# Sums of x one or two splits sooner, an earlier stage-end read-out, and a sixth pair of blocks in seven products

## The chip, the cores and the metric

The kernel runs on one core of one Trainium2 chip. The metric is the device time of one execution, in microseconds (us); the kernel is judged by the median of its runs. The engines are called PE (TensorE, matrix products), PEld (its weight loads), DVE (VectorE), ACT (ScalarE), POOL (GpSimd) and SP (SyncE, which issues most transfers).

## The reference

Two layers (DEPTH = 2) of a token mixer work on x of 256 tokens by 2048 channels in float32. Per layer:

```
h = rmsnorm(x, norm_g)
c_a, c_glu, c_gate, q_down, kv_down, k_pe, m_gate, g_conv, g_mla = split(h @ w_in)
y_conv = conv_branch(c_a, c_glu, c_gate, ...) @ w_proj_conv     # GLU, causal depthwise conv, layernorm, silu, gate
y_mla  = mla_branch(q_down, kv_down, k_pe, m_gate, ...) @ w_proj_mla   # low-rank attention, 16 heads, gate
y = sigmoid(g_conv) * y_conv + sigmoid(g_mla) * y_mla
x = x + y @ w_out
```

All that the change touches are the products by `w_proj_conv` and `w_out` (2048 by 2048 each) and what is done to their results.

## The kernel before, in words

**Blocks and splits.** Every weight matrix is cut into blocks of 512 columns (a few are narrower). A stage is named for its matrix: the last stages of a layer are gmla, gconv, pmla, pconv (`w_proj_conv`) and wout (`w_out`), four blocks each. A block of pconv or wout has 2048 rows of weights, in eight pieces of two groups of 128 rows (KS = 2). Float32 accuracy is made out of a faster float format (fp32r): each weight piece `raw` is copied to a rounded high part `hi` by ACT (a CAST), and DVE subtracts to get the low part `lo`; the activations are kept as high and low parts as well. One piece then takes three products (high by high, low of x by high, high of x by low), for two groups of rows and two tiles of 128 tokens: twelve matmuls of 512 columns. This piece of work, the making of its parts with it, is called a split here (a tick in the code). DVE makes low parts two splits ahead of PE, ACT high parts three ahead (LO_AHEAD, HI_AHEAD), and SP loads further ahead into seven `raw` buffers.

**Seven products.** Some pairs of blocks save products. For the first two pieces of both blocks of a pair, that is four weight pieces (b11 and b21 of the left block, b12 and b22 of the right one) and two tiles of tokens, the eight piece-by-tile products are replaced by seven products of sums (Strassen's scheme in Winograd's form). Their weight sides are pieces or sums of pieces: q1 = b11, q2 = b21, q3 = b22, q7 = b12 + b22, q6 and q4 of further sums, q5 = b12 and b11 combined; DVE makes these sums (`sum`, `form`). Their x sides are tiles of x or sums of tiles, called forms in the code: `form_a` and `form_b`. One such product takes six matmuls. The remaining six pieces of each block are plain splits, so a pair has twelve splits, first the left block's and then the right one's; for wout's first pair the order alternates by twos. The set SEVEN names the pairs: pconv 2 (that is blocks 2 and 3), wout 0 and wout 2, in both layers, without wout 2 in the last layer: five pairs. A pair's products are spread out by `plan_all`: q1, q7, q6 and q5 go ahead of the splits that lie 7, 5, 3 and 2 from the end of the block or pair before it (TAIL), and q2, q4 and q3 ahead of splits 0, 2 and 4 of the pair itself.

**The order of the work.** Each engine's order is fixed by hand: the class `InOrder` chains every instruction to the one issued before it on its engine. `product` walks through a block's splits. For each it issues the products of the seven that stand there, prepares parts of coming weights (`prepare`), issues the twelve matmuls and then calls `background`, which counts a clock of splits up by one and issues all steps that are due. `at_slot(n, f)` makes f due n splits later, and there is no waiting for a step's data in it: a step that is issued with its data not there holds up its engine's queue.

**The sums of x.** `make_forms` plans four steps: `whole` (DVE adds high and low parts to whole numbers, two adds, tiles `whole_a` and `whole_b`), one split later `differences` (four DVE subtractions), one later `separate` (ACT's high parts of the forms) and one later DVE's low parts. `forms_at` says when the first is due, in splits from the start of the block in which the seven begin: `ticks + TAIL[ticks][1] - 3`, where `TAIL[ticks][1]` is the place of q7, the first that needs a form. For a block of eight splits that is 0, for a pair of twelve it is 4. It is called once for each stage and layer: for pconv (whose products begin in pconv block 1, of eight splits) and for wout (which begin in the pconv pair, of twelve), so four times in all. Where the number is 0 or less, the steps are planned one block sooner, during the block before.

**The read-out.** A finished block is read out of the accumulators by an evacuation function (`pconv_evac`, `wout_evac`), issued as a step of `background`. If a pair of seven products begins inside the block (`planned.begins`), the two token tiles are read out at EVAC_AT = 1 split after the last one and one later; otherwise both are read out together, EVAC_AT splits after the last one, or at `evac_at` for the last half of a block or pair. `evac_at` was 0 for `i == 3`, a block that a pair of seven products never has as its own index. In `pconv_evac` and `wout_evac` (layer 0) a result is then turned: written to DRAM in strips (`park`, on POOL's queue, for the last block's second tile on SP's), fetched back (`fetch`, POOL) and transposed in blocks by DVE, at fixed numbers of splits after the read-out, and split into high and low parts for the next stage (`yT`, `hT`). In the last layer `wout_evac` adds x and sends the result to the output.

**The end.** The last block of the last layer, wout 3, has eight plain splits in `last_product`: the two last splits are reordered so that token tile 0 finishes first and is read out, then tile 1 without its last piece, and this last piece is made in two halves of 256 columns in banks of their own (`acc_end`), each added and sent off as soon as it is there. x for a block comes by `wout_begin`, at the block's start, or for the second block of a pair at slot 8.

Of the kernel before, what the change touches and what calls it, by code (L numbers as in the profile page):

```python
# [11 lines left out]
F32 = mybir.dt.float32  # L12
# [57 lines left out]

REVOLUTION_PIECES = 6

SEVEN = {(l, kind, i) for l in range(DEPTH) for kind, i in (("pconv", 2), ("wout", 0), ("wout", 2))} - {(DEPTH - 1, "wout", 2)}


def revolution_pieces():
# [43 lines left out]
def trunk(ctx: ExitStack, tc: tile.TileContext, xT, x, g_in, pos, win, wuq, wukv, wpc, wpm, wo, cst, rows, invf, out):  # L120
# [281 lines left out]
            return high(0, 0) + high(1, 0) + low(0) + low(1) + high(0, 1) + high(1, 1)  # L402
        return [e for t in two for p in two for e in high(t, p)] + low(0) + low(1)

    def last_product(planned, stat, first_out, early_out, half_out):

        nk, n, mine = planned.nk, planned.n, [tick[-1][1] for tick in planned.ticks]
        blocks_begun[0] += 1
        own, other = blocks_begun[0] % 2, 1 - blocks_begun[0] % 2
        pts = [acc_p.tile([P, 512], F32, tag=f"acc{own}{t}", name=f"acc{mine[0]}_{t}") for t in range(T)]  # L410
        ends = [acc_p.tile([P, 256], F32, tag=f"acc{other}{a}", name=f"acc{mine[0]}_end{a}") for a in range(2)]

        def products(j, t, dst, cols, begin, end):
            hi, lo, _ = done[mine[j]]
            terms = [(kk, p) for p in range(2) for kk in range(KS)] + [(kk, 2) for kk in range(KS)]
            for m, (kk, part) in enumerate(terms):
                sh, sl = stat(j * KS + kk, t)
                stationary, w = ((sh, hi), (sl, hi), (sh, lo))[part]
                pe.matmul(
                    dst, stationary, w[:, kk, cols],  # L420
                    start=begin and m == 0, stop=end and m == len(terms) - 1,
                )

        whole = slice(0, n)
        for j, i in enumerate(mine):
            prepare(i)
            if j < len(mine) - 2:
                for t, kk, part in order_of_products(i, False, False):
                    k = j * KS + kk
                    sh, sl = stat(k, t)  # L430
                    stationary, w = ((sh, done[i][0]), (sl, done[i][0]), (sh, done[i][1]))[part]
                    pe.matmul(pts[t], stationary, w[:, kk, :], start=k == 0 and part == 0, stop=False)
            elif j == len(mine) - 2:
                products(j, 0, pts[0], whole, False, False)
                products(j + 1, 0, pts[0], whole, False, True)
                first_out(pts[0])
                products(j, 1, pts[1], whole, False, True)
                early_out(pts[1])
            else:
                for a in range(2):  # L440
                    products(j, 1, ends[a], slice(256 * a, 256 * a + 256), True, True)
                    half_out(a, ends[a])
            background(n)

    def prepare(i):
        for a in range(HI_AHEAD + 1):
            split_hi(i + a)
            if a <= LO_AHEAD:
                split_lo(i + a)
        form(i + HI_AHEAD + 1)  # L450
# [85 lines left out]
        at_slot(begin + 2, separate, 0.0, 1.0)  # L536
        return forms

    def product(planned, stat, evacuate, evac_at=EVAC_AT, costs=(0.0, 0.0), before=None, tardy=None):
        nk, n = planned.nk, planned.n  # L540
        seven = planned.seven
        if seven:
            dst = [[seven.banks[q] for q in qs] for qs in (("q1", "q7"), ("q6", "q5"))]
        else:
            dst = [accumulators(f"acc{planned.pieces[0]}")]

        def evac(right, ts=range(T)):
            for t in ts:
                evacuate(*((right,) if seven else ()), t, dst[right][t][:, : 2 * n] if n == PAIRED else dst[right][t][:, :n])

        ends = {}
        for at, tick in enumerate(planned.ticks):
            ends[tick[-1][0]] = at
        for at, tick in enumerate(planned.ticks):
            for q, i, of in tick[:-1]:
                prepare(i)
                one_of_seven(q, i, of)
            right, i, j = tick[-1]
            pts = dst[right]
            final = at == ends[right]  # L560
            prepare(i)
            hi, lo, _ = done[i]
            if before:
                before(j)
            begins = j == 0 and not seven
            for t, kk, part in [(t, kk, p) for t in range(T) for p in range(2) for kk in range(KS)] if n == PAIRED else ():
                k = j * KS + kk
                pe.matmul(
                    pts[t][:, : (n if part else 2 * n)], stat(k, t)[part], hi[:, kk, :] if part else pairs_of[i][:, kk, :],
                    start=k == 0 and part == 0, stop=k == nk - 1 and part == 1,  # L570
                )
            for t, kk, part in () if n == PAIRED else order_of_products(i, final, j == tardy):
                k = j * KS + kk
                sh, sl = stat(k, t)
                stationary, w = ((sh, hi), (sl, hi), (sh, lo))[part]
                pe.matmul(
                    pts[t][:, :n], stationary, w[:, kk, :],
                    start=begins and kk == 0 and part == 0, stop=k == nk - 1 and part == 2,
                    skip_group_check=seven is not None,
                )  # L580
            if final and planned.begins:
                half = tuple(c / 2 for c in costs)
                for t in range(T):
                    steps.insert(t, (clock[0] + 1 + EVAC_AT + t, half, lambda right=right, t=t: evac(right, [t])))
            elif final:
                steps.insert(0, (clock[0] + 1 + (EVAC_AT if at < len(planned.ticks) - 1 else evac_at), costs, lambda right=right: evac(right)))
            background(n, [u for _, u, _ in tick[:-1]])
# [203 lines left out]
    for l in range(DEPTH):  # L791
# [660 lines left out]
        def add_out(t, c, s, ps, xt, engine):  # L1452
            vec.tensor_add(xt[:, s], ps, xt[:, s])
            engine.dma_start(out[t, :, c * 512 + s.start : c * 512 + s.stop], xt[:, s])

        def wout_end(pl, stat, c=3, keep=keep, add_out=add_out):
            xts = [keep.pop(("x", c, t)) for t in range(T)]
            halves = [slice(a, a + 256) for a in (0, 256)]

            last_product(  # L1460
                pl, stat,
                lambda ps: add_out(0, c, slice(0, 512), ps, xts[0], sp),
                lambda ps: vec.tensor_add(xts[1], ps, xts[1]),
                lambda a, ps: add_out(1, c, halves[a], ps, xts[1], (act, sp)[a]),
            )

        def wout_evac(c, t, ps, keep=keep, l=l, last_layer=last_layer):
# [41 lines left out]
        for at_block, (kind, i, pl) in enumerate(planned):  # L1509
# [4 lines left out]

            def forms_at(b):
                ticks = len(planned[b][2].ticks)
                return ticks + TAIL[ticks][1] - 3

            of, after = pl.begins, at_block + 1 + bool(pl.seven)
            if of:  # L1520
# [49 lines left out]
            elif kind == "mgate":  # L1570
                product(pl, uses_h, lambda t, ps, i=i: mgate_evac(i, t, ps), costs=(0.0, 3.5))
            elif kind == "gmla":
                product(pl, uses_h, lambda t, ps, i=i: gmla_evac(i, t, ps), costs=(0.0, 2.7))
            elif kind == "pmla":
                product(pl, stat_of(*keep["o"]), lambda t, ps, i=i: pmla_evac(i, t, ps), costs=(1.25, 0.0))
            elif kind == "gconv":
                product(pl, uses_h, lambda t, ps, i=i: gconv_evac(i, t, ps), costs=(0.0, 3.9))
            elif kind == "cgate":
                product(pl, uses_h, lambda t, ps, i=i: cgate_evac(i, t, ps), costs=(0.0, 2.0))
            elif kind == "pconv":  # L1580
                while "yc" not in keep:
                    run_fill()
                product(pl, stat_of(*keep["yc"]), evac_of(pconv_evac, i, pl), 0 if i == 3 else EVAC_AT, (2.4, 0.0),
                        before=before_pconv if i == 0 else None)
            else:
                if i:
                    wout_begin(i)
                else:
                    at_slot(5, lambda f=wout_begin: f(0))
                if pl.seven:  # L1590
                    at_slot(8, lambda i=i, f=wout_begin: f(i + 1))
                if last_layer and i == 3:
                    wout_end(pl, stat_of(*keep["y"]))
                    continue
                product(pl, stat_of(*keep["y"]), evac_of(wout_evac, i, pl),
                        0 if i == 3 else EVAC_AT, (1.25, 1.5), tardy=6 if i == 0 else None)
        if not last_layer:
            h_hi, h_lo = keep["h"]

# [105 lines left out]
```

## Time and profile before

| | |
|---|---|
| median of 3 runs | 1876.45 us (1876.35 to 1877.25) |
| the profiled execution, its own time | 1876.67 us |
| its span, first to last instruction | 1874.8 us |
| granted TensorE clock, mean | 1.000 |
| instructions | 26919 |
| DMA | 445.03 MB, mean 237 GB/s |

The profile is of one execution. The share of busy time of an engine is an average; PE's is taken with modelled ends of its matmuls, which overlap, so that the starts of matmuls tell more than their ends. A row of a timeline reads: start, duration of the group, engine, line, operation, result<-operands and shape, how many, and in brackets the idle time of the engine before it with what ended it. All instructions have the line L131, that of the helper which records the order of issue; one goes by the tiles' names. `acc`, `left` and `right` are accumulators (the latter two of the blocks of a pair), `hT`, `ycT` and `yT` the inputs of the stages that read h, the conv branch and y.

### The profile page before, as it was taken

The page shows a single profiled execution, that of the slowest core. Times are in us where ns is not written, and L with a number is a line of the kernel's source. Part 1 is how long each engine was busy: PE and PEld are TensorE (multiplying, and loading weights), DVE is VectorE, ACT ScalarE, POOL GpSimd, SP SyncE. Part 2 cuts the span into 40 slices and gives each one's busy share as a digit, 9 for nine tenths or more (in the row PEclk, how much of TensorE's full clock was granted, in tenths as well). Part 3 has the DMA queues.
Part 4 walks back from the last instruction along what each step waited for, and adds up shares of the span by engine and source line. Part 5 has one row for each costly group of instructions (what it writes and reads, how often), then busy time and mean ns, then how long its engine had stood idle before and what let it go on. Part 6 is the DMA issues. An engine that isn't in the chain of part 4 may idle for free.

```text
span 1874.8 us, 26919 instructions
## 1 busy us (share of the span) xinstructions
PE 1863.2 (99%) x8419; PEld 1550.6 (83%) x8419; DVE 1657.2 (88%) x2560; ACT 1370.2 (73%) x2454; POOL 493.1 (26%) x942
## 2 busy tenths in 40 slices
PE   9999999999999999999999999999999999999999
PEld 8888888888888888778888888888888888887787
DVE  6999998898999999899769998888899999896974
ACT  7678888888887766555657689788889877564552
POOL 0155555542200000111421555555322000001210
PEclk9999999999999999999999999999999999999999
DMA  8777877887765566577977787777877556665684
GB/s 330 237 262 254 270 251 246 269 275 226 241 204 195 194 215 213 179 230 251 315 251 233 257 269 261 254 252 259 270 229 248 193 195 206 197 220 190 221 292 139
DMA packets 138959, 445.03 MB, mean 237 GB/s; under 512 B 23680, under 2 KB 29056, under 8 KB 138816
## 3 DMA queue, kind: packets, MB, share of 16 engines
q1 hardware_dynamic: 104976, 359.50, 57.9%
q0 software_dynamic: 32832, 82.62, 13.7%
q8 instruction: 66, 1.08, 0.2%
q10 hardware_dynamic: 1008, 1.20, 0.2%
q14 instruction: 77, 0.63, 0.1%
HBM read 399.18 MB, written 44.04 MB: 236 GB/s over the span
## 4 chain that ended last, share of the span: by engine, by line
PE 98%; DMA 1%; DVE 1%; issue 0%; POOL 0%; ACT 0%; DVEq 0%; POOLq 0%
PE acc L131 84%; PE left L131 6%; PE right L131 5%; PE o_ps L131 1%; PE s1w L131 1%; PE s L131 1%; DMA turned<-turn_d 0%; DVE sum L131 0%; DMA turn_d<-xres 0%; DMA gx<-in_g 0%; DMA x_in<-in_xT 0%; DVE lo L131 0%; DVE form_a L131 0%; POOL turn_d L131 0%; PE acc_end L131 0%
## 5 line engine op out<-in xcount | busy, mean ns | idle before, releaser
L131 ACT CAST hi<-raw 128x1024 fp32r<-128x1024 f32 (+2 forms) x683 | 698.9, 1029 | 354.4 <-PE acc L131 241.8
L131 DVE TENSOR_TENSOR lo<-raw,hi 128x1024 fp32r<-128x1024 f32 (+2 forms) x667 | 802.2, 1205 | 125.6 <-PE acc L131 62.7
L131 PE MATMUL acc<-hi,hT 128*128 128x512 f32 (+1 forms) x1728 | 422.0, 384 | 0.5 <-ACT hT L131 0.5
L131 PEld LDWEIGHTS acc<-hi,hT 128*128 128x128 f32 x1728 | 319.5, 188 | 64.6 <-ACT hT L131 0.9
L131 PE MATMUL acc<-hi,h_hi 128*128 128x512 f32 (+1 forms) x864 | 264.2, 387 | 0.4 <-ACT h_hi L131 0.4
L131 PE MATMUL acc<-hi,h_lo 128*128 128x512 f32 (+2 forms) x864 | 260.0, 382 | 0.0
L131 ACT ACTIVATE tap<-u_t,cst 128x256 f32<-128x256 f32 x522 | 227.4, 499 | 4.4 <-DVE v_t L131 3.9
L131 PE MATMUL acc<-lo,h_hi 128*128 128x512 f32 (+1 forms) x832 | 224.6, 386 | 0.0
L131 PE MATMUL acc<-lo,hT 128*128 128x512 f32 (+1 forms) x832 | 224.0, 386 | 0.0
L131 POOL DMA_DIRECT2D turned<-turn_d x88 | 49.3, 561 | 535.8 <-DVE v_t L131 337.6
L131 DVE SCALAR_TENSOR_TENSOR v_t<-u_t,cst,v_t 128x256 f32<-128x256 f32 x438 | 187.5, 479 | 2.4
L131 PEld LDWEIGHTS acc<-hi,h_lo 128*128 128x128 f32 x864 | 161.5, 188 | 32.9 <-DVE h_lo L131 0.2
L131 DVE TENSOR_TENSOR v_t<-v_t,tap 128x512 f32<-128x512 f32 x261 | 179.5, 688 | 8.5
L131 PEld LDWEIGHTS acc<-hi,h_hi 128*128 128x128 f32 x864 | 160.1, 188 | 31.4 <-ACT h_hi L131 0.8
L131 POOL DMA_DIRECT2D turn_d<-gate x184 | 100.1, 551 | 317.1 <-DVE gate L131 202.4
L131 PEld LDWEIGHTS acc<-lo,h_hi 128*128 128x128 f32 x832 | 155.1, 188 | 31.5 <-DVE lo L131 0.3
L131 PEld LDWEIGHTS acc<-lo,hT 128*128 128x128 f32 x832 | 155.2, 188 | 31.1
L131 PE MATMUL acc<-hi,oT 128*128 128x512 f32 x512 | 127.8, 389 | 0.0
L131 PE MATMUL acc<-hi,qkc 128*128 128x512 f32 x448 | 115.4, 389 | 0.0
L131 PEld LDWEIGHTS acc<-hi,oT 128*128 128x128 f32 x512 | 95.8, 188 | 19.7
L131 PEld LDWEIGHTS acc<-hi,qkc 128*128 128x128 f32 x448 | 83.6, 188 | 17.0
L131 POOL DMA_DIRECT2D turn_d<-su x128 | 69.9, 552 | 99.6 <-DVE su L131 89.4
(242 smaller groups left out, 2436.1 us busy)
## 6 DMA issues: line engine op xcount, KB each, us to landing
raw<-in_win SPq DMA_DIRECT2D x397, 512.0 KB, 4.3
raw<-in_wpm SPq DMA_DIRECT2D x64, 512.0 KB, 3.4
raw<-in_wpc SPq DMA_DIRECT2D x64, 512.0 KB, 3.4
raw<-in_wo SPq DMA_DIRECT2D x64, 512.0 KB, 4.9
raw<-in_wukv SPq DMA_DIRECT2D x32, 512.0 KB, 4.3
turned<-turn_d POOLq DMA_DIRECT2D x56, 256.0 KB, 4.9
raw<-in_wuq SPq DMA_DIRECT2D x24, 512.0 KB, 4.5
turn_d<-qk POOLq DMA_DIRECT2D x128, 96.0 KB, 3.8
```

Source lines behind the costliest of these rows:

```text
L131: ins = getattr(self.engine, name)(*a, **k)
```

## The change

Three edits. First, `forms_at` gives a number two lower for a block of eight splits (-2 in place of 0) and one lower for a pair of twelve (3 in place of 4). Second, `evac_at` is 0 where `i + bool(pl.seven) == 3`, so for the last pair of a stage too. Third, wout 2 of the last layer joins SEVEN as a sixth pair; since `last_product` knew only plain blocks, its ending becomes a function `closing` that `product` calls for the last two splits, with the same three kinds of pieces and the two halves in the banks `acc00` and `acc01`.

```diff
-SEVEN = {(l, kind, i) for l in range(DEPTH) for kind, i in (("pconv", 2), ("wout", 0), ("wout", 2))} - {(DEPTH - 1, "wout", 2)}
+SEVEN = {(l, kind, i) for l in range(DEPTH) for kind, i in (("pconv", 2), ("wout", 0), ("wout", 2))}
...
-    def last_product(planned, stat, first_out, early_out, half_out):
...
+    def closing_of(stat, first_out, early_out, half_out):
+
+        def closing(step, last_two, pts):
+            pieces = [(done[i], j) for _, i, j in last_two]
...
+            whole = slice(0, 512)
+            if step == 0:
+                products(pieces[0], 0, pts[0], whole, False, False)
+                products(pieces[1], 0, pts[0], whole, False, True)
                 first_out(pts[0])
+                products(pieces[0], 1, pts[1], whole, False, True)
                 early_out(pts[1])
             else:
+                halves = [acc_p.tile([P, 256], F32, tag=f"acc0{a}", name=f"acc_end{a}") for a in range(2)]
                 for a in range(2):
+                    products(pieces[1], 1, halves[a], slice(256 * a, 256 * a + 256), True, True)
+                    half_out(a, halves[a])
...
+            if closing and at >= len(planned.ticks) - 2:
+                prepare(i)
+                closing(at - len(planned.ticks) + 2, [tick[-1] for tick in planned.ticks[-2:]], pts)
+                background(n)
+                continue
...
             def forms_at(b):
                 ticks = len(planned[b][2].ticks)
-                return ticks + TAIL[ticks][1] - 3
+                return ticks + TAIL[ticks][1] - (5 if ticks == 8 else 4)
...
-                product(pl, stat_of(*keep["yc"]), evac_of(pconv_evac, i, pl), 0 if i == 3 else EVAC_AT, (2.4, 0.0),
+                product(pl, stat_of(*keep["yc"]), evac_of(pconv_evac, i, pl), 0 if i + bool(pl.seven) == 3 else EVAC_AT, (2.4, 0.0),
...
-                if last_layer and i == 3:
-                    wout_end(pl, stat_of(*keep["y"]))
-                    continue
-                product(pl, stat_of(*keep["y"]), evac_of(wout_evac, i, pl),
-                        0 if i == 3 else EVAC_AT, (1.25, 1.5), tardy=6 if i == 0 else None)
+                stat = stat_of(*keep["y"])
+                product(pl, stat, evac_of(wout_evac, i, pl), 0 if i + bool(pl.seven) == 3 else EVAC_AT, (1.25, 1.5),
+                        tardy=6 if i == 0 else None, closing=wout_end(stat) if last_layer and i + bool(pl.seven) == 3 else None)
```

More of the change, by code (lines that the diff above doesn't have):

```diff
@@ L403, in order_of_products @@
         return [e for t in two for p in two for e in high(t, p)] + low(0) + low(1)
-    def last_product(planned, stat, first_out, early_out, half_out):
[L407 to L435, printed above, removed]
@@ new lines, in closing_of, with products @@
+    def closing_of(stat, first_out, early_out, half_out):
+        def closing(step, last_two, pts):
+            pieces = [(done[i], j) for _, i, j in last_two]
+            def products(piece, t, dst, cols, begin, end):
+                (hi, lo, _), j = piece
+                terms = [(kk, p) for p in range(2) for kk in range(KS)] + [(kk, 2) for kk in range(KS)]
+                for m, (kk, part) in enumerate(terms):
+                    sh, sl = stat(j * KS + kk, t)
+                    stationary, w = ((sh, hi), (sl, hi), (sh, lo))[part]
+                    pe.matmul(
+                        dst, stationary, w[:, kk, cols],
+                        start=begin and m == 0, stop=end and m == len(terms) - 1, skip_group_check=not begin,
+                    )
+            whole = slice(0, 512)
+            if step == 0:
+                products(pieces[0], 0, pts[0], whole, False, False)
+                products(pieces[1], 0, pts[0], whole, False, True)
@@ L436, in last_product @@
                 first_out(pts[0])
-                products(j, 1, pts[1], whole, False, True)
+                products(pieces[0], 1, pts[1], whole, False, True)
                 early_out(pts[1])
             else:
+                halves = [acc_p.tile([P, 256], F32, tag=f"acc0{a}", name=f"acc_end{a}") for a in range(2)]
                 for a in range(2):
-                    products(j, 1, ends[a], slice(256 * a, 256 * a + 256), True, True)
-                    half_out(a, ends[a])
-            background(n)
+                    products(pieces[1], 1, halves[a], slice(256 * a, 256 * a + 256), True, True)
+                    half_out(a, halves[a])
@@ L445, in prepare @@
+        return closing
     def prepare(i):
@@ L537, in make_forms, with product @@
         return forms
-    def product(planned, stat, evacuate, evac_at=EVAC_AT, costs=(0.0, 0.0), before=None, tardy=None):
+    def product(planned, stat, evacuate, evac_at=EVAC_AT, costs=(0.0, 0.0), before=None, tardy=None, closing=None):
         nk, n = planned.nk, planned.n
@@ L1454, in add_out, with wout_end @@
             engine.dma_start(out[t, :, c * 512 + s.start : c * 512 + s.stop], xt[:, s])
-        def wout_end(pl, stat, c=3, keep=keep, add_out=add_out):
-            xts = [keep.pop(("x", c, t)) for t in range(T)]
+        def wout_end(stat, c=3, keep=keep, add_out=add_out):
             halves = [slice(a, a + 256) for a in (0, 256)]
[L1460 to L1464, printed above, removed]
+            xt = lambda t: keep["x", c, t]
+            return closing_of(
+                stat,
+                lambda ps: add_out(0, c, slice(0, 512), ps, xt(0), sp),
+                lambda ps: vec.tensor_add(xt(1), ps, xt(1)),
+                lambda a, ps: add_out(1, c, halves[a], ps, xt(1), (act, sp)[a]),
             )
```

## The prediction

> **What bounds the kernel now.** I read the page first, then the engine waits of PE, then the timeline around each wait.
>
> ```profile
> span 1874.8 us, 26919 instructions
> ...
> PE 1863.2 (99%) x8419; PEld 1550.6 (83%) x8419; DVE 1657.2 (88%) x2560; ACT 1370.2 (73%) x2454; POOL 493.1 (26%) x942
> ...
> PEclk9999999999999999999999999999999999999999
> ...
> PE left L131 <- DVE form_a L131: 6.6, 4, 2.1
> ...
> PE acc L131 <- ACT hT L131: 0.5, 1, 0.5
> PE acc L131 <- ACT h_hi L131: 0.4, 1, 0.4
> ```
>
> The reader is to see three things. PE is busy for 1863.2 of 1874.8 us and its granted clock is full in every slice, so time comes off only by fewer matmuls or fewer stalls of PE. The list of stalls is short: four of them, 6.6 us together, on `form_a`, a sum of x for the seven products; one of 0.5 us on `hT`, the input of layer 1; one of 0.4 us at the start. DVE and ACT have 88% and 73%, so they matter only where they hand something to PE late. A stall costs more than its listed idle time, because the modelled ends of the matmuls hide a part, so I price stalls by starts of matmuls. First the unit, from the timeline of the pconv pair of layer 0:
>
> ```profile
> 825.83 1.98 PE L131 MATMUL left<-hi,ycT 128*128 128x512 f32 x8
> ...
> 828.55 1.07 PE L131 MATMUL right<-hi,form_b 128*128 128x512 f32 x4
> ...
> 832.63 1.07 PE L131 MATMUL left<-hi,yT 128*128 128x512 f32 x4
> ...
> 833.99 1.52 PE L131 MATMUL left<-hi,ycT 128*128 128x512 f32 x6
> ```
>
> A plain split, twelve matmuls of 512 columns, runs from 825.83 to 828.55: 2.72 us, 0.227 us a matmul. One of the seven products, six matmuls, runs from 832.63 to 833.99: 1.36 us. Any longer stretch of the same count is a stall.
>
> **Part 1, the sums of x sooner.** In the timeline ahead of the pconv pair of layer 0 (the products are begun inside pconv block 1, eight splits):
>
> ```profile
> 777.50 1.23 DVE L131 TENSOR_TENSOR lo<-raw,hi 128x1024 fp32r<-128x1024 f32 x1 [1.50 <-PE acc L131]
> ...
> 784.08 0.69 DVE L131 TENSOR_TENSOR whole_a<-ycT,ycT 128x512 f32<-128x512 f32 x1
> ...
> 790.59 0.42 DVE L131 TENSOR_TENSOR whole_b<-whole_a,whole_b 128x256 f32<-128x256 f32 x1
> ...
> 792.31 1.22 DVE L131 TENSOR_TENSOR lo<-raw,hi 128x1024 fp32r<-128x1024 f32 x1
> ...
> 794.01 1.07 PE L131 MATMUL acc<-lo,ycT 128*128 128x512 f32 x4
> ...
> 794.92 0.61 PE L131 MATMUL left<-hi,form_a 128*128 128x512 f32 x2
> ...
> 796.85 0.68 DVE L131 TENSOR_TENSOR form_a<-whole_a,form_a 128x512 fp32r<-128x512 f32 x1
> ...
> 797.59 0.73 PE L131 MATMUL left<-hi,form_a 128*128 128x512 f32 x2 [2.05 <-DVE form_a L131]
> ...
> 798.62 1.99 PE L131 MATMUL acc<-hi,ycT 128*128 128x512 f32 x8
> ```
>
> Product q7 starts at 794.92 with the high part of `form_a`, waits for the low part, which DVE begins only at 796.85, and the next split starts at 798.62: 3.70 us in place of 1.36, a loss of 2.34. The plan put that subtraction into the background of the split just ahead of q7, at the end of a DVE queue that was still working. And for wout, ahead of its first pair (begun inside the pconv pair, twelve splits):
>
> ```profile
> 839.24 0.69 DVE L131 TENSOR_TENSOR gate<-left,sc 128x512 f32<-128x512 f32 x1
> 839.43 0.61 PE L131 MATMUL left<-hi,form_a 128*128 128x512 f32 x2
> ...
> 840.57 0.68 DVE L131 TENSOR_TENSOR form_a<-whole_a,form_a 128x512 fp32r<-128x512 f32 x1
> ...
> 841.31 0.73 PE L131 MATMUL left<-hi,form_a 128*128 128x512 f32 x2 [1.27 <-DVE form_a L131]
> ...
> 842.34 1.99 PE L131 MATMUL right<-hi,ycT 128*128 128x512 f32 x8
> ```
>
> From 839.43 to 842.34 are 2.91 us in place of 1.36, a loss of 1.55. Here DVE first reads out the left half (`gate`, from 839.24) and only then makes the low part. Layer 1 has the same two places: the four stalls of the list are 6.6 us, twice 2.05 + 1.27. So sums of x cost PE 2 x (2.34 + 1.55) = 7.8 us.
>
> With the change the four steps (add, differences, high parts, low parts) keep their distance to each other and come two splits sooner in the first place, one in the second. First place: the low parts are now due one split after pconv block 0, behind that block's read-out, where the differences stand today; they are two subtractions of 0.68 in place of four of 0.42. By today's clock that queue would be through with them at about 792.0 (790.59 + 1.4), and q7 asks with its third matmul, at 795.37, so 3 us are to spare and all 2.34 go. The adds and differences move into the last three splits of pconv block 0, where DVE idles 1.50 us before a low part (row 777.50); two adds of 0.69 and four differences of 0.42 nearly fit in that, and what doesn't is drawn from the lead of two splits with which low parts are made. Second place: the low parts move ahead of the low part of the next weight, the sum for q6 and the read-out, 1.2 + 1.2 + 1.3 us of queue; they would begin about 836.9 (840.57 less 3.7) and be done about 838.2, 1.7 us before q7's third matmul at 839.88, so all 1.55 go. I charge nothing for the moved steps: they are the same instructions, none of them issues a DMA, and POOL's and SP's queues are not passed. If that cover failed, the price is the rival below.
>
> What is late next? In the first place the low part of the weight ahead of q7 (792.31 + 1.22 = 793.53) is used at 794.01, 0.48 us later; it gains 0.3, since shorter work stands ahead of it. In the second place DVE is nearly full until the end of the pair:
>
> ```profile
> 836.00:872.00 36.00, 34.73 (x153) 28.45 (x152) 34.91 (x41) 19.24 (x22) 8.79 (x16) 1.00 0.69 215
> ...
> 867.62 2.35 DVE L131 TENSOR_TENSOR lo<-raw,hi 128x1024 fp32r<-128x1024 f32 x2
> ...
> 871.37 1.07 PE L131 MATMUL right<-lo,yT 128*128 128x512 f32 x4
> ```
>
> 34.91 of 36 us are busy, so DVE will not run sooner when PE does, and each margin behind the stall shrinks by 1.55. The thinnest that I find is a low part done at 868.84 (867.62 + 1.22) and used at 871.37: 2.53 falls to 1.0, still positive.
>
> The Trainium skill ("TensorE: Matmul & The Clock Gate", the queue depths under the array's architecture) says that VectorE is a strict first-in first-out queue while PE may pull weight loads ahead. The rows agree for VectorE: the subtraction at 840.57 stood behind the read-out at 839.24 though its inputs were long there. Taken alone that rule speaks against the change too, as every step put ahead delays all behind it; it is the first rival.
>
> **Part 2, the read-out at the stage's end.** The argument that becomes 0 is used only where no seven-product pair follows; behind the pconv pairs the other branch with its fixed distance is taken, and the last layer has its own ending. So one place moves: the end of wout in layer 0.
>
> ```profile
> 937.55 1.98 PE L131 MATMUL acc<-hi,hT 128*128 128x512 f32 x8
> ...
> 938.95 1.28 DVE L131 TENSOR_TENSOR xres<-right,xres 128x512 f32<-128x512 f32 x2
> ...
> 952.31 0.71 DVE L131 STREAM_TRANSPOSE turned<-turned 128x512 f32<-128x512 f32 x1 [2.40 <-DMA turned<-turn_d]
> ...
> 953.87 0.61 PE L131 MATMUL acc<-hi,hT 128*128 128x512 f32 x2
> ...
> 954.95 0.79 PE L131 MATMUL acc<-hi,hT 128*128 128x512 f32 x2 [0.46 <-ACT hT L131]
> ...
> 960.28 1.98 PE L131 MATMUL acc<-hi,hT 128*128 128x512 f32 x8
> ```
>
> The read-out (938.95) starts a chain through DRAM that ends in transposes at 952.31 and in `hT`, for which PE waits at 954.95. The two splits from 953.87 to 960.28 take 6.41 us, 0.97 over 2 x 2.72. The read-out moves ahead of one low part, to the end of PE's last split, behind which layer 1 starts at 937.55: some 1.4 us sooner; the parks on POOL and SP and the fetch on POOL move with it. The 2.40 us for which DVE stands at the transpose get longer by about 1, with low parts of weights queued behind, but these have two splits of lead. Bounds: 0.97 gained, or as much lost if those low parts come late. I take 0.9 gained.
>
> **Part 3, the sixth pair.** Seven products in place of eight: 42 matmuls for 48, 6 x 0.227 = 1.36 us less of PE. By the Trainium skill (the same page, "Wait — 56ns, not 53.3ns?") a warm matmul of 512 columns takes 215.7 ns start to start; by that it would be 1.29, and the 0.227 of the rows decides. DVE and ACT get more work there: three more low parts and four sums of 1.22 us (row 877.21), and four joins of about 0.69 (as the read-out at 839.24): 11.3 us.
>
> ```profile
> 1828.00:1868.00 40.00, 40.00 (x178) 33.14 (x177) 19.77 (x22) 13.16 (x13) 4.26 (x8) 1.00 0.48 149
> ...
> 877.21 1.23 DVE L131 TENSOR_TENSOR sum<-raw,raw 128x1024 f32<-128x1024 f32 x1 [2.10 <-DMA raw<-in_wo]
> ...
> 880.09 1.21 DVE L131 TENSOR_TENSOR lo<-sum,hi 128x1024 fp32r<-128x1024 f32 x1
> ...
> 884.06 0.61 PE L131 MATMUL left<-lo,form_a 128*128 128x512 f32 x2
> ...
> raw<-in_wo SPq DMA_DIRECT2D x64, 512.0 KB, 4.9
> ...
> xres<-x_dram SPq DMA_DIRECT2D x8, 256.0 KB, 6.3
> ...
> DMA to landing us min/median/max: 1.9/4.8/10.4
> ```
>
> DVE is busy for 19.77 of 40 us in the last 40 us of today's plain blocks; 11.3 us more fit. The ending itself has the same matmuls (twelve whole, six whole, twelve halves) in banks that are free by then: 0. One step is new on the path: x for the last block is asked for at slot 8, three splits or 8.2 us ahead of the first read-out. The median landing is 6.3 us, the longest of `xres` 10.4: 0 to 2.2 us of cost, and I take 0, as SP issues ahead of PE.
>
> **The sum.** 7.8 + 0.9 + 1.4 = 10.1 us. The profiled execution took 1876.67 us (span 1874.8 and 1.9 around it): 1866.6. The median of the runs is 0.2 lower: 1866.4.
>
> **The rivals.** (1) The stall moves to a weight's low part in the pconv pairs. For: DVE at 34.91 of 36. Against: 1.0 us of margin is left. If the margin is overdrawn, at most 1.55 in each layer comes back: 1866.4 + 3.1 = 1869.5. Chance 0.11. (2) The change doesn't do what it says: the steps are due sooner in the plan, but DVE, being behind, reaches them no sooner. For: its load. Against: two read-outs and weights are passed in the queue itself. Only parts 2 and 3 would count: 1876.4 - 2.3 = 1874.1, no measurable change. Chance 0.05. (3) Slower: the new pair starves for weights. Its first sum needs two pieces of block 3 during block 1. In layer 0 that sum already waited 2.10 us for `raw` (877.21); its low part was done at 881.30 and used at 884.06, 2.8 us later. If in the last layer, where x and out travel too, all four extra pieces landed one after the other, that is 4 x 4.9 = 19.6 us, 16.8 beyond the margin: 1883.2. It outweighs the gain from 10.1 us beyond the margin on. Against: layer 0 has the same loads at the same distance, with the next layer's behind them, and PE did not wait. Chance 0.04.
>
> **The numbers.** 0.80 for the forecast, whose own range is 1865.4 to 1868.6 (1.0 below for the spread of the runs shown, 1876.35 to 1877.25, and 2.2 above for x). With the first rival the range is 1865.4 to 1870.0. A measurement of this kernel tells about 0.2%, 3.75 us, from no change; the forecast and rival (1) lie beyond it: faster 0.91, same 0.05, slower 0.04.
>
> **What would show it.** Right: the line `form_a` is gone from PE's waits, each q7 takes 1.36 us from start to start, PE has 8413 matmuls, and the two splits that took 6.41 take about 5.5. Wrong: PE waits on `lo` from DVE between the sums and the end of the pconv pairs (rival 1), still on `form_a` (rival 2), on `lo` or a sum behind `raw` in the last 50 us (rival 3), or DVE's last additions wait for `xres`.

## The result, and the profile after

The changed kernel takes 1866.8 us (median of 4 runs, 1866.56 to 1867.27) against 1876.85 us of the kernel before in the same session (4 runs, 1876.35 to 1877.98). The ratio is 0.9946, with a 95% interval of 0.9929 to 0.9963: faster by about 10 us, 0.5%. The forecast was 1866.4. The profiled execution took 1866.75 us. In one later session a single execution of the kernel before took 3822.62 us, about twice as long as every other one, and no ratio and no count below contains it.

The page of the changed kernel, and below it its list of PE's waits (us in total, times, longest):

```profile
span 1865.0 us, 26913 instructions
...
PE 1859.9 (100%) x8413; PEld 1549.2 (83%) x8413; DVE 1666.2 (89%) x2571; ACT 1372.7 (74%) x2459; POOL 495.9 (27%) x942
```

```profile
PE right L131 <- DVE xres L131: 0.8, 1, 0.8
PE warm L131 <- PEq L1687: 0.8, 1, 0.8
PE acc L131 <- ACT hi L131: 0.2, 1, 0.2
```

PE has six matmuls fewer, `form_a` and `hT` are gone from its waits, and one line is new: the right block of a pair waits for `xres`. First the place where the sums of x were late, ahead of the pconv pair of layer 0, in the timeline of the changed kernel:

```profile
789.30 0.69 DVE L131 TENSOR_TENSOR gate<-gate,ym 128x512 f32<-128x512 f32 x1
789.91 0.69 DVE L131 TENSOR_TENSOR form_a<-whole_a,form_a 128x512 fp32r<-128x512 f32 x1
...
794.24 1.07 PE L131 MATMUL left<-hi,form_a 128*128 128x512 f32 x4
...
795.14 0.62 PE L131 MATMUL left<-lo,form_a 128*128 128x512 f32 x2
795.60 0.62 PE L131 MATMUL acc<-hi,ycT 128*128 128x512 f32 x2
...
833.61 0.68 DVE L131 TENSOR_TENSOR form_a<-whole_a,form_a 128x512 fp32r<-128x512 f32 x1
...
836.39 1.07 PE L131 MATMUL left<-hi,form_a 128*128 128x512 f32 x4
...
837.30 0.62 PE L131 MATMUL left<-lo,form_a 128*128 128x512 f32 x2
837.75 1.07 PE L131 MATMUL right<-hi,ycT 128*128 128x512 f32 x4
```

The low part of `form_a` now stands right behind the read-out (`gate`) and is done at 790.60; q7 asks for it with its third matmul, at 794.69, 4 us later. q7 runs from 794.24 to 795.60, 1.36 us, where it took 3.70. The second place, ahead of wout's first pair, has the low part done at 834.29, and q7 runs from 836.39 to 837.75, again 1.36. In layer 1 both places look the same.

The end of layer 0, same view:

```profile
932.96 1.30 PE L131 MATMUL acc<-hi,hT 128*128 128x512 f32 x5
933.15 1.29 DVE L131 TENSOR_TENSOR xres<-right,xres 128x512 f32<-128x512 f32 x2 [1.49 <-PE right L131]
...
946.72 0.71 DVE L131 STREAM_TRANSPOSE turned<-turned 128x512 f32<-128x512 f32 x1 [3.81 <-DMA turned<-turn_d]
...
949.27 1.07 PE L131 MATMUL acc<-hi,hT 128*128 128x512 f32 x4
...
954.74 1.52 PE L131 MATMUL acc<-hi,hT 128*128 128x512 f32 x6
```

The read-out comes 0.19 us behind the start of layer 1, before it was 1.40. DVE stands 1.4 us longer at the transpose (3.81 for 2.40), and the two splits from 949.27 to 954.74 take 5.47 us in place of 6.41: no wait is left. And the end of the kernel, same view:

```profile
1857.18 0.61 PE L131 MATMUL right<-lo,yT 128*128 128x512 f32 x2
1857.83 0.69 DVE L131 TENSOR_TENSOR xres<-right,xres 128x512 f32<-128x512 f32 x1 [4.16 <-PE right L131]
...
1858.58 1.19 PE L131 MATMUL right<-hi,yT 128*128 128x512 f32 x4 [0.78 <-DVE xres L131]
...
1861.70 0.42 DVE L131 TENSOR_TENSOR xres<-acc_end,xres 128x256 f32<-128x256 f32 x1 [0.22 <-PE acc_end L131]
```

This is the new line of the waits. Two matmuls begin at 1857.18 and the next ones at 1858.58: 1.40 us for 0.45, with 0.11 more in the first matmul behind it: 1.05 us lost. PE goes on when DVE has read token tile 0 out, though it next writes token tile 1.

**Where the 9.8 us of the span come from.** One stretch belongs to no edit: the start. The same group of matmuls, ahead of any edited work, begins 0.68 us later in the profile of before than after; first before, then after:

```profile
741.88 1.98 PE L131 MATMUL acc<-hi,oT 128*128 128x512 f32 x8
```

```profile
741.20 1.98 PE L131 MATMUL acc<-hi,oT 128*128 128x512 f32 x8
```

From there to the end of the span it is 1132.9 us before and 1123.8 after, a gain of 9.1: 7.78 from q7, 0.97 from `hT`, 1.36 from six matmuls, less 1.05 at the end, which is 9.06.

### The profile page after: what moved, and what is told of

Its sections match the earlier page's. It is cut to its first block, busy times and chain, and to the rows that moved or that the text cites. A ratio compares the mean times of both kernels' runs of the same rounds, so it can differ in the third digit from the quotient of the medians.

```text
span 1865.0 us, 26913 instructions
## 1 busy us (share of the span) xinstructions
PE 1859.9 (100%) x8413; PEld 1549.2 (83%) x8413; DVE 1666.2 (89%) x2571; ACT 1372.7 (74%) x2459; POOL 495.9 (27%) x942
## 4 chain that ended last, share of the span: by engine, by line
PE 100%; DMA 0%; DVE 0%; ACT 0%; issue 0%
PE acc L131 83%; PE left L131 7%; PE right L131 7%; PE o_ps L131 1%; PE s1w L131 1%; PE s L131 1%; DMA raw<-in_win 0%; PE acc_end L131 0%; DVE xres L131 0%; ACT hi L131 0%; PE var L131 0%; PE mu L131 0%
```

## The experiments

Two sessions were run, on different chips, each with the kernel before beside the experiments. The theory is the prediction's three parts, and for the end of the kernel this: the right block's two accumulators are one double PSUM tile (`pair`), so that the order of issue makes the writing of tile 1 wait for the reading of tile 0. The rivals are in each expectation.

**One part alone (e1_sums, e2_readout, e3_sixth).** The kernel before with the first edit; the kernel before with the second; the changed kernel with these two put back.

```diff
e1_sums (kernel before)
-                return ticks + TAIL[ticks][1] - 3
+                return ticks + TAIL[ticks][1] - (5 if ticks == 8 else 4)
e2_readout (kernel before; wout's line, and the same in pconv's)
-                        0 if i == 3 else EVAC_AT, (1.25, 1.5)
+                        0 if i + bool(pl.seven) == 3 else EVAC_AT, (1.25, 1.5)
e3_sixth (changed kernel: these lines as before)
```

> The kernel before with the sums of x sooner and nothing else. Theory (the four stalls on form_a were all of it, and nothing takes their place): 7.8 us less than before, no line form_a among PE's waits, the wait of 0.5 us on hT still there. Rival (the changed kernel owes part of this to the other two edits, or the stalls come back on the low parts of weights): less than 6 us, and PE waits on lo.

> The kernel before with the stage-end read-out in the last split and nothing else. Theory: only the read-out of wout's last pair in layer 0 moves, the wait on hT goes, 0.9 to 1.0 us less; the four waits on form_a stay at 6.6 us. Rival (the longer stand of DVE at the transpose makes low parts of weights late): the time is the same or up to 1 us more, and PE waits on lo near the start of layer 1.

> The change with the sums of x and the read-out put back: the sixth pair with its ending alone. Theory (six matmuls less are 1.36 us, the new wait on xres at the end takes 1.05 back): 0.3 us less than before, with a wait PE right <- DVE xres of 0.8 us. Rival (the wait at the end comes from the other edits): 1.4 us less, and no such wait.

Measured, against a kernel before of 1877.36 us: e1 1868.43 us (1867.93 to 1868.80), ratio 0.9954 (0.9941 to 0.9967); e2 1876.49 (1874.96 to 1877.24), ratio 0.9995 (0.9986 to 1.0004); e3 1876.75 (1875.11 to 1879.47), ratio 0.9999 (0.9990 to 1.0008). PE's waits of e1, then of e3:

```profile
PE acc L131 <- ACT hT L131: 0.6, 1, 0.6
```

```profile
PE left L131 <- DVE form_a L131: 6.6, 4, 2.1
PE right L131 <- DVE xres L131: 0.8, 1, 0.8
```

e1 loses `form_a` and keeps `hT`; e2 loses `hT` and keeps `form_a` (6.6 us); e3 keeps `form_a` and has the new `xres`. One line doesn't fit: e3 reads out as late as before and yet has no line `hT`. It still loses something there, by starts of matmuls 0.47 us over the same two splits, where before loses 0.97 and e1 1.33. DVE's stand at the transpose, which the way through DRAM ends, goes with it, 1.90, 2.40 and 2.86 us; e3's row, then e1's:

```profile
953.20 0.71 DVE L131 STREAM_TRANSPOSE turned<-turned 128x512 f32<-128x512 f32 x1 [1.90 <-DMA turned<-turn_d]
```

```profile
948.49 0.71 DVE L131 STREAM_TRANSPOSE turned<-turned 128x512 f32<-128x512 f32 x1 [2.86 <-DMA turned<-turn_d]
```

From the read-out to this transpose it takes 12.9 us in e3, 13.4 in before and 13.8 in e1. So the loss at `hT` differs between executions, with the time that the way through DRAM takes; why that differs is open.

By the same group of matmuls as above (741.51 in e1) the rest of e1's span is 1867.0 - 741.5 = 1125.5 us, 7.4 less than before. By starts of matmuls e1 gains 3.9 us in each layer at the sums of x, and gives 0.4 to 0.5 back at its longer wait for `hT`; so the theory's 7.8 holds. In e2's profile the two splits take 5.44 us, nothing over 2 x 2.72. The medians of e2 and e3 do not tell half a microsecond, because their executions spread over 2 to 4 us, while those of e1 lie within 0.9. What spreads them shows in e2's profile: a stretch at a lower clock. Its timeline behind the first stall, and its windows ahead of, behind and well behind it (the number after the busy times is the granted clock):

```profile
796.86 0.74 PE L131 MATMUL left<-hi,form_a 128*128 128x512 f32 x2 [2.05 <-DVE form_a L131]
...
798.15 3.33 PE L131 MATMUL acc<-hi,ycT 128*128 128x512 f32 x8
801.32 1.09 PE L131 MATMUL acc<-lo,ycT 128*128 128x512 f32 x4
```

```profile
790.00:796.00 6.00, 4.81 (x22) 3.65 (x20) 5.90 (x8) 2.58 (x4) 4.36 (x8) 1.00 0.63 160
797.70:801.20 3.50, 3.50 (x10) 2.75 (x9) 3.12 (x3) 1.03 (x1) 0.56 (x1) 0.53 0.91 328
802.00:806.00 4.00, 4.00 (x19) 3.30 (x18) 1.97 (x2) 1.67 (x2) 0.00 (x0) 1.00 0.63 210
```

The eight matmuls from 798.15 take 3.17 us; in the profile of before the same eight, behind the same stall of 2.05, take 1.82. The matmuls begin 0.427 us apart for 3.4 us, in place of 0.227: eight of them cost 1.6 us more. In e3's profile it happened behind both stalls of 2.05. Of 34 executions of the kernel before in the two sessions, 12 have a mean clock of 1.000 and take 1875.47 to 1876.32 us, 19 have 0.999 and take 1877.15 to 1878.66, 3 have 0.998 and take 1879.10 to 1879.36. Of these only the mean clock is known. By an estimate from e2's profile, a stretch of 3.4 us at a clock of 0.53 takes 0.0009 off the mean, so 0.999 is read here as one such stretch and 0.998 as two. Among the executions with a mean clock of 1.000, e2 takes 1874.96 to 1875.15, 0.7 to 0.9 less than the mean of before's, 1875.86 (0.9 was the term), and e3 1875.11 to 1876.25, on the mean 0.4 less (1.36 less 1.05 would be 0.3). That fits the two terms; it does not prove them to a tenth.

**The end of the kernel (e4_two_tiles, e7_late_first).** The changed kernel with the right block's two accumulators in two PSUM tiles and the left block's in the double one; and with the accumulators as they are, but the read-out of token tile 0 issued behind the products of tile 1.

```diff
e4_two_tiles
-            pair = tp_p.tile([P, 2, 512], F32, tag="tp", name="right")
-            c12, c22 = pair[:, 0], pair[:, 1]
-            c11 = s_p.tile([P, 512], F32, tag="s0", name="left0")
-            c21 = extra_p.tile([P, 512], F32, tag="extra", name="left1")
+            pair = tp_p.tile([P, 2, 512], F32, tag="tp", name="left")
+            c11, c21 = pair[:, 0], pair[:, 1]
+            c12 = s_p.tile([P, 512], F32, tag="s0", name="right0")
+            c22 = extra_p.tile([P, 512], F32, tag="extra", name="right1")
e7_late_first
-                first_out(pts[0])
                 products(pieces[0], 1, pts[1], whole, False, True)
+                first_out(pts[0])
```

> The changed kernel, with the accumulators of the second set of banks dealt out otherwise: the right block's two token tiles get two PSUM tiles of their own, the left block's two share the double one. Theory (PE waits at the end because both token tiles of the right block are one tile, so that writing one waits for the reading of the other): the wait PE right <- DVE xres is gone and the kernel takes 1.0 us less than the changed one, 1865.8. Rival (PE waits for the read-out itself, whatever the tiles): the wait stays and the time is that of the changed kernel, 1866.8. Also open: the left block could get such a wait in its place, on rest or xres.

> The changed kernel with the accumulators as they are, but at the end the read-out of token tile 0 issued behind the six matmuls of tile 1, not ahead of them. Theory (PE waited only since the write to the second half of the double tile came behind a read of the first): no wait PE right <- DVE xres, 1.05 us less on PE, 0.3 us given back by DVE's later additions, 1866.1. Rival (PE waits for the banks whatever the order): 1866.8 or more.

Measured: e4 1866.15 us (1865.80 to 1866.45), ratio to before 0.9942 (0.9929 to 0.9955); e7 1866.37 (1866.15 to 1866.58), ratio 0.9943 (0.9930 to 0.9955). Timeline of e4, then of e7:

```profile
1857.71 0.62 PE L131 MATMUL right<-lo,yT 128*128 128x512 f32 x2
1858.16 1.07 PE L131 MATMUL right<-hi,yT 128*128 128x512 f32 x4
1858.36 0.69 DVE L131 TENSOR_TENSOR xres<-right,xres 128x512 f32<-128x512 f32 x1 [4.16 <-PE right L131]
```

```profile
1858.67 0.62 PE L131 MATMUL right<-lo,yT 128*128 128x512 f32 x2
1859.12 0.64 PE L131 MATMUL acc_end<-hi,yT 128*128 128x256 f32 x4
1859.32 1.29 DVE L131 TENSOR_TENSOR xres<-right,xres 128x512 f32<-128x512 f32 x2 [5.52 <-PE right L131]
```

In e4 the matmuls of tile 1 begin at 1858.16, 0.45 behind the two before them, while DVE is yet to read tile 0 (1858.36). In e7 PE doesn't wait either, and both tiles are read in one go. So the wait is the shared tile's and not one on a result: two ways of parting the write from the read remove it. From the common group (741.72 in e4, 741.34 in e7) to the end it is 1123.0 and 1123.1 us, 0.8 and 0.7 less than the changed kernel, which is less than the 1.0 expected of e4. PE gets all of it back: up to the start of its last matmul e4 gains 1.07 us and e7 1.10. But from there to the end e4 takes 3.84 us and e7 4.00, the changed kernel 3.61; in e7 DVE's last additions come later behind PE, in e4 the additional time lies behind DVE's last addition, and its cause is open. e4 is the best version found. None of its five runs is as long as the shortest of the changed kernel, but the two were timed in different sessions and the intervals of their ratios overlap, so the profile rows, not the medians, carry this.

**How many splits sooner (e5_one_split).** The changed kernel with the sums of x only one split sooner in the first place as well.

```diff
-                return ticks + TAIL[ticks][1] - (5 if ticks == 8 else 4)
+                return ticks + TAIL[ticks][1] - 4
```

> The changed kernel with the sums ahead of pconv one split sooner instead of two (wout's as in the change). Theory (by the changed kernel's rows the low parts would be done about 793.6, 1.1 us ahead of q7's third matmul at 794.7): no wait on form_a, the time of the changed kernel, 1866.8. Rival (the second split is needed, as pconv block 0's read-out stands ahead): waits on form_a of 0.5 us or more in each layer, 1868 or more.

Measured, against 1877.66 us of before in the second session: 1867.03 us (1866.86 to 1867.48), ratio 0.9947 (0.9934 to 0.9959). `form_a` is not among PE's waits. In the first place:

```profile
792.14 0.68 DVE L131 TENSOR_TENSOR form_a<-whole_a,form_a 128x512 fp32r<-128x512 f32 x1
...
794.07 1.07 PE L131 MATMUL left<-hi,form_a 128*128 128x512 f32 x4
```

The low part is done at 792.82, 1.7 us ahead of q7's third matmul at 794.52 (1.1 was expected). The second split in the first place buys nothing that these runs show; the first one is enough.

**The cover in DVE (e6_ballast).** The changed kernel with eight idle additions of 128x256 on DVE, due eight splits into each pconv pair. They add to a tile `idle` that nothing uses; the two lines that make and clear it at the kernel's start are not shown here, nor in e8.

```diff
             elif kind == "pconv":
+                if pl.seven:
+                    def ballast():
+                        for _ in range(8):
+                            vec.tensor_add(idle[:, :], idle[:, :], idle[:, :])
+                    at_slot(8, ballast)
```

> The changed kernel with eight idle additions of 128x256 (0.42 us each, 3.4 us) put into DVE's queue behind split 7 of the pconv pair of both layers; nothing reads them. Theory (DVE is full there, and the low parts behind it have 1.8 to 2.0 us of margin in the changed kernel): PE waits on lo, 1.4 to 1.6 us in each layer, 1869.6 to 1870.0. Rival A (there is no cover): 6.8 us more, 1873.6. Rival B (DVE catches up ahead of PE): the time of the changed kernel.

Measured: 1872.44 us (1871.70 to 1872.92), ratio 0.9975 (0.9965 to 0.9984), 5.6 us more than the changed kernel. PE's waits of e6, and the timeline of layer 0:

```profile
PE right L131 <- DVE lo L131: 2.9, 2, 1.5
...
PE right L131 <- DVE rest L131: 0.6, 2, 0.3
```

```profile
842.99 3.64 DVE L131 TENSOR_TENSOR idle<-idle 128x256 f32<-128x256 f32 x8
...
846.54 1.22 DVE L131 TENSOR_TENSOR lo<-raw,hi 128x1024 fp32r<-128x1024 f32 x1
...
847.82 1.19 PE L131 MATMUL right<-lo,ycT 128*128 128x512 f32 x4 [1.46 <-DVE lo L131]
```

The load pushes the low part behind it to 846.54, and PE stands 1.46 us for it; by starts of matmuls 1.73 us are lost there. In the changed kernel the low part of that place is done 2.0 us ahead of its use, and the load of 3.64 less this cover is 1.64. That is the theory. Not foreseen was about 1.2 us more in each layer further back, most of it in wout's first pair (`rest` and a low part, at 885 to 892 us in layer 0), 40 us later, so DVE had not caught up by then. With it the time is outside the theory's 1869.6 to 1870.0 and nearer rival A's 1873.6; the rows decide against rival A, since the first wait is 1.46 us and not the whole load. Rival (1) of the prediction is a real mechanism, 2 us of DVE's work away.

**Do the stalls bring the half clock? (e8_longer_stalls).** The kernel before with four idle additions ahead of the low parts of each of the four forms.

```diff
-            at_slot(1, lambda: [vec.tensor_sub(l, z, h.bitcast(F32)) for l, z, h in subs], 1.3)
+            def lows():
+                for _ in range(4):
+                    vec.tensor_add(idle[:, :], idle[:, :], idle[:, :])
+                for l, z, h in subs:
+                    vec.tensor_sub(l, z, h.bitcast(F32))
+            at_slot(1, lows, 1.3)
```

> The kernel before with four idle additions of 128x256 (0.42 us each, 1.7 us) ahead of the low parts of the sums of x, so that each of the four stalls of PE gets 1.7 us longer. Theory (the stretches of half clock of 3.4 us that follow a stall of 2.05 us in some executions, and cost 1.6 us each, come from the length of PE's idle time): 6.8 us for the stalls and 1.6 us for half clock behind nearly every one of them, about 1889, mean clock 0.996. Rival (those stretches come by chance, however long the stall): 6.8 us and as few of them as before, 1882.5 to 1884.

Measured: 1888.3 us (1887.06 to 1889.27), ratio 1.0058 (1.0045 to 1.0072). PE's waits of e8, and its window behind the first stall:

```profile
PE left L131 <- DVE form_a L131: 13.5, 4, 3.8
```

```profile
798.90:802.20 3.30, 3.30 (x9) 2.63 (x10) 2.80 (x4) 1.04 (x1) 0.00 (x0) 0.55 0.58 164
```

The stalls grew by 6.9 us, the time by 12.4 over the 1875.9 us of before's executions at full clock. The other 5.5 us are put down to the clock: all five executions have a mean of 0.996 or 0.997, and the profile shows half clock behind the first three of the four stalls, behind the third for twice 3.4 us. By starts of matmuls these four stretches cost 5.9 us in the profile. The rival, in which the half clock has nothing to do with the stall, falls.

## Why the prediction was right, point by point

**The sums of x: right.** Forecast 7.8 us, measured 7.78 by starts, 7.4 with this edit alone. The reason held too: the steps had their inputs long before and stood behind other work in DVE's queue. The 3 and 1.7 us that it would have to spare became 4.1 (790.60 to 794.69) and 2.6 (834.29 to q7's third matmul at 836.84). Rival (2), that DVE would reach the steps no sooner, did not come. What the prediction did not ask is how little would do; e5 shows that one split does.

**The margins: right in kind, wrong in size.** It took all margins in the pair to shrink by 1.55 and the thinnest to fall from 2.53 to 1.0. In the changed kernel:

```profile
827.78 2.35 DVE L131 TENSOR_TENSOR lo<-raw,hi 128x1024 fp32r<-128x1024 f32 x2
...
830.50 0.62 PE L131 MATMUL left<-lo,yT 128*128 128x512 f32 x2
...
863.74 2.35 DVE L131 TENSOR_TENSOR lo<-raw,hi 128x1024 fp32r<-128x1024 f32 x2
...
866.77 1.07 PE L131 MATMUL right<-lo,yT 128*128 128x512 f32 x4
```

The low part it named is done at 863.74 + 1.22 = 864.96 and used at 866.77: 1.81 us. DVE did run a little sooner when PE did, so it shrank by 0.7 and others behind the second stall by up to 1.2. The thinnest lies elsewhere, 1.50 us (829.00 to 830.50), at a low part that the sums now stand ahead of; its margin was 3.2 before. Rival (1) did not come, and e6 prices it.

**The read-out: right, its size in part by luck.** 0.9 forecast, 0.94 to 0.97 measured; DVE stands 1.4 us longer at the transpose, and no low part came late for it. The forecast and the measure both take the loss from one profile of before. Without the edit it was 0.47 us in e3 and 1.33 in e1, so the edit is worth what the execution before would have lost, and a forecast to a tenth was not to be had from one profile.

**The sixth pair: the six matmuls right, the ending wrong.** 1.36 us came off. The step that failed is "the same matmuls ... in banks that are free by then: 0". Its term is 1.05 us. The banks were free, but the right block's two accumulators were parts of one tile, and the program keeps the order between a tile's reader and its next writer for the whole tile: e4 and e7. None of the signs of being wrong that it lists names this wait. The cost that it did foresee, 0 to 2.2 us for x, was 0. The tile `xres` from 1700 us on, in the changed kernel (count, durations of the issue, first and last start):

```profile
L131 SPq DMA_DIRECT2D xres<-x_dram x8: 327/381/423, 1796.0 to 1836.9; - x8
...
DMA to landing us min/median/max: 1.9/4.5/7.7
```

The last x is asked for at 1836.9, 21 us ahead of its first use at 1857.83, and no transfer of the tile takes over 7.7 us. Rival (3) did not come either; PE waits for no weight in the last 50 us.

**The sum.** 10.1 us were forecast, 9.1 are the change's, and 0.68 us came from a start that was slower in the profile of before. These two errors, 1.05 and 0.68, have opposite signs, and by luck the forecast came closer than its steps were. The medians hide a third: by their mean clocks, before's executions lose 1.6 us or more to the half clock in about two of three, which neither the sum nor its profile contained. Against before's executions at full clock (1875.9) the changed kernel gains 9.1 us, as the profiles say; against its median 10.0.

## What to carry to other kernels

On an engine that works its queue in order, a small step which another engine waits for belongs ahead of long work, as soon as its inputs exist; one split was enough here, and the price is a thinner margin for all that stands behind it, to be measured by a deliberate load. When a block changes the accumulators that it ends in, look at which of them share a tile, not only at whether the banks are free. Before comparing two kernels to a microsecond, set aside the start and count the stretches at half clock, by starts of matmuls in both traces.

## What the runs showed of the hardware

A stall of PE of 2.05 us (2.44 us from start to start of two matmuls that otherwise lie 0.227 apart) can bring TensorE's clock down to half for 3.4 us, at 0.427 us from start to start of a 512-column matmul in place of 0.227, and it costs about 1.6 us beyond the stall. The granted clock was 0.53 in 3.5 us of e2 that hold such a stretch. In the profiles of before, e2 and e3 it followed three of the six stalls of 2.05 us; by their mean clocks, 22 of 34 executions of the kernel before had at least one such stretch. What decides which stalls are followed by it is open. Stalls of 3.0 and 3.8 us did so in three of four places of e8's profile. Those of 1.27 us (the second place, in the profiles of before, e2 and e3) and of 1.46 us (e6) were not followed by it; the 30 executions of e1, e4, e5, e6 and e7, in whose profiles no stall is longer, all have a mean clock of 1.000. The Trainium skill ("TensorE: Matmul & The Clock Gate", the table under "What's actually happening") puts the fall to half clock behind an idle window of about 3.4 us, and under "Why this matters for your kernels" it advises against idle gaps over about 3 us. That doesn't agree with this case: here 2.05 us is enough at times. The same table puts the return to full clock behind a busy window of about 3.4 us; the length of the half-clock stretch agrees with that.

The start differs between executions, too: the matmul at 741.88 us in the profile of before comes between 741.0 and 741.9 in the profiles of all these kernels, though no edit touches the work ahead of it.
